# A hand-written opening order with x in half PSUM tiles, and two later due times around the first mixer

## The chip, the cores and the metric

The kernel runs on one core of a Trainium2 chip. The metric is the device time of one execution in microseconds (us). Before the change three runs took 948.01, 948.50 and 948.53 us, median 948.50. The core's engines are TensorE (PE; its weight loads are listed apart as PEld), VectorE (DVE), ScalarE (ACT), GpSimd (POOL) and SyncE (SP), which issues most DMA transfers. Each engine takes its own instructions strictly in the order in which the program lists them; a semaphore makes an instruction, and all that stand behind it on its engine, wait for a result of another engine or for a DMA.

## The reference, cut to what matters

Two layers over x (256 tokens x 1024), each a half-step feed-forward network, a mixer, and a second half-step feed-forward network:

```python
for i in range(2):
    h = rmsnorm(x, ffn1_norm[i])
    x = x + 0.5 * (silu(h @ w_gate) * (h @ w_up)) @ w_down          # D_FF = 2816
    h = rmsnorm(x, mix_norm[i])
    q_s, k_s, v_s, q_m = split(h @ w_in[i])                         # 12 + 12 + 12 + 4 heads of 64
    k_m, v_m = split(rmsnorm(mem, mem_norm[i]) @ w_mem_kv[i])       # memory keys and values
    q, k = rmsnorm(q_s, ...), rmsnorm(k_s, ...)                     # per head; the same for q_m, k_m
    o_s = chunked attention with bias (i = 0) or differential attention with rotary (i = 1)
    o_m = softmax(q_m k_m^T / 8) v_m
    x = x + concat(o_s, o_m) @ w_out[i]
    x = x + 0.5 * swiglu(rmsnorm(x, ffn2_norm[i]), ...)             # as the first
```

All of it is float32, to float32 accuracy.

## The kernel before, in words

**Arithmetic.** Each float32 operand is split in two: `hi`, its rounding to the type fp32r (a copy on ACT), and `lo`, the rest (a subtraction on DVE). A float32 product is three matmuls: hi·xh (line 542), lo·xh (545) and hi·xl (548), in `dense`. The left operand is x transposed, 128 features by 128 tokens (`xh`, `xl`), the right one a weight block of 128 x 512.

**Weights.** `loader` brings them from DRAM in chunks of 128 x 2048 (four k-tiles of 128 x 512), each into one of three `raw` buffers, by DMAs on SP's queue (line 321). `split_hi` (line 367) and `split_lo` (line 385) make `hi` and `lo` from them, into four pairs of buffers. The chunks are called W0, W1, W2, ... here, in order of use. W0 comes in eight pieces, W1 in four, each later gate/up chunk in two of 512 KB. The items of W0 and W1 are split k-tile by k-tile, later gate/up items two k-tiles at a time (`w` in `Item`). W0, W1 and W2 hold 24 matmuls each: four k-tiles, two blocks of 128 tokens, three matmuls. W36 to W39 are the weights of the memory keys and values, W40 and W41 those of the first query/key block of `w_in` in layer 0, W42 and W43 its value block, W44 and W45 its second query/key block.

**Order of the work.** A planner in the kernel's Python (`Flow`) sets it at build time: it keeps an expected time of PE (`flow.now`) and of ACT, DVE and POOL, and runs generators that issue an instruction when its inputs are expected to be there. `yield flow.now + 5.0` means: expect this in 5 us. The result is a fixed list for each engine; the expected times exist only while it is built. A step expected too early stands too early in the list, and its engine then waits at it.

**The opening** (lines 1751 to 1787). x is 2 blocks of tokens (`tb`) by 2 halves of 512 features (`hf`). `start(tb, hf, t)` puts `prep_half` into the plan: four transposes by PE into one PSUM tile (line 578), a scaling by the norm's gain on DVE over 128 x 512 (line 612), the rounding on ACT (line 650: `xh`), the rest on DVE (line 654: `xl`). `start_gain` transposes the gain row (line 1762; tile `gps`, copied to `gcol` at line 1764). `warm(n)` puts matmuls without use on PE (line 1778), of the 128 x 128 identity, which POOL makes first. `square` and `prep_rstd` compute the norm's factor for each token, needed first at the evacuation of the first gate/up block (line 728).

**The first mixer.** `memory_kv` projects the memory keys, normalises them (`kmn`), turns them with a DVE transpose and a round trip through DRAM (`kb` to `kd`, back as `kr`, SP lines 1064 and 1069) and splits them into `km`: two ACT instructions (line 1192) and four DVE ones (line 1195) for each layer. `proj(0)` makes the first query/key block in PSUM tiles `pj`. `head_norm` squares it on ACT (line 1040), sums on DVE (`hss`), takes a power on POOL (`hf`, line 585) and scales on DVE (`qkn`, line 1049). `qk_evac` then turns `qkn` on PE into the tile `qktp` (line 578). Scores are the tile `S` (line 1487), softmax is `pe`, its transposes `ptp`, the product with the values `AV`, and the output projection `acc`. POOL meanwhile works through some ninety small operations for the rotary tables of layer 1 (`ropew`), which end in two sines on ACT (lines 1281 and 1282) and an exponential (line 1321); DVE's `ropeC`, `ropeS` and `nlam` need those.

Of the kernel before, what the change touches and what calls it, by code (L numbers as in the profile page):

```python
# [12 lines left out]
F32 = mybir.dt.float32  # L13
# [28 lines left out]
T_TR = 0.107  # L42
SLACK = 0.4
AHEAD = 0


class Flow:
# [10 lines left out]
        (self.idle if idle else self.threads).append([self.now, gen])  # L58

    def pe(self, dur):  # L60
        self.now += dur
        return self.now + HOP

    def eng(self, e, dur):
# [103 lines left out]
def kernel(  # L168
# [10 lines left out]
    nc = tc.nc  # L179
# [23 lines left out]
    def bank(name, shape=(P, 4, P)):  # L203
        return banks.take(list(shape), F32, name)
# [67 lines left out]
    class Item:  # L272
# [3 lines left out]
        def __init__(self, raws, uses=8, w=1):  # L276
            self.raws, self.uses = raws, uses
            self.hi = self.lo = None
            self.hit, self.lot, self.st = [None] * 7, [None] * 7, [None] * 4
            self.n, self.frees, self.takes, self.gives, self.guest = 1, 1, 0, 0, False  # L280
            self.sums, self.t = [], []
            self.index = len(items)
            w = 1 if len(items) < 2 else w
            self.units = [(self.own(q, w), q, w, None) for q in range(0, 4, w)]
            items.append(self)

# [25 lines left out]
    def loader():  # L312
        for i, c in enumerate(chunks):
            yield lambda: raw_left[0] > 0
            raw_left[0] -= 1
            c.raw = wraw.tile([P, 2048], F32, tag="raw", name=f"raw{i}")
            dma_free[0] = max(dma_free[0], flow.now)
            n = len(c.parts)
            lat = LAT + slow[0] if i > 1 else 0.6
            for j, (dst, src) in enumerate(c.parts):  # L320
                (nc.scalar if i == 0 and j == 1 else nc.sync).dma_start(out=dst(c.raw), in_=src)
                dma_free[0] += 3.0 / n
                if i < 2 and j % 2:
                    for q in range((j - 1) * 4 // n, (j + 1) * 4 // n):
                        c.block[q] = dma_free[0] + lat
# [4 lines left out]
            c.arrive = dma_free[0] + lat  # L330
# [17 lines left out]
    def split_hi():  # L348
        for i, it in enumerate(items):
            yield lambda: (hl_left[0] >= it.n and all(r.raw is not None for r in it.raws)  # L350
                           and (xt_room[0] or not it.guest))
            hl_left[0] -= it.n
            if it.guest:
                xt_room[0] = False
            yield max(r.block[0] for r in it.raws)
            it.hi, it.lo = ([whl.tile([P, 2048], F32R, tag=x, name=f"{x}{i}_{j}") for j in range(it.n)]
                            for x in ("hi", "lo"))
            if it.guest:
                for x, ts in (("xh", it.hi), ("xl", it.lo)):
                    ts += [xtp.tile([P, KT, P], F32R, tag=f"{x}{j}", name=f"g{x}{j}") for j in range(2)]  # L360
            for src, q, w, dep in it.units:
                yield max(r.arrive if dep is not None else r.block[q + w - 1] for r in it.raws)
                if dep is not None:
                    yield lambda: it.st[dep] is not None
                    yield it.st[dep]
                yield calm_a(i)
                nc.scalar.copy(out=it.part(0, q, w), in_=src())  # L367
                t = flow.act(512 * w)
                it.hit[q:q + w] = [t] * w

    def split_lo():
        for i, it in enumerate(items):
            if it.sums:
                yield lambda: all(r.raw is not None for r in it.raws) and g2.left >= it.takes + 2
                yield max(r.arrive for r in it.raws)
                it.t += [g2.take([P, 512], F32, "wsum") for _ in range(it.takes)]
                for j, (x, y) in enumerate(it.sums):
                    yield calm_v(i)
                    nc.vector.tensor_sub(it.t[j], x(), y())  # L379
                    it.st[j] = flow.dve(512)  # L380
            for src, q, w, dep in it.units:
                yield lambda: it.hit[q] is not None
                yield it.hit[q]
                yield calm_v(i)
                nc.vector.tensor_sub(it.part(1, q, w), src(), it.part(0, q, w).bitcast(F32))  # L385
# [84 lines left out]

    def plan_ffn(l, nm, wg, wu, wd):
        def parts(g, c):
            pieces = (4, 2)[len(chunks)] if len(chunks) < 2 else 1
            a = cols4(wg[l], c, g * 256, 256, 0, pieces)
            b = cols4(wu[l], c, g * 256, 256, 256, pieces)
            return [q for ab in zip(a, b) for q in ab]
# [680 lines left out]
    def memory_kv(l):  # L1157
# [7 lines left out]
        def evac(ps, tb, t):  # L1165
            yield t
            nat = yield from head_norm(ps[:, 0:256], 4, mrs[tb], "kmn")
            nc.scalar.activation(vm[:, tb, :], ps[:, 256:512], AF.Copy, scale=mrs[tb])
            kvt[1][tb] = flow.act(256)
            banks.give()  # L1170
            if tb == 0:
                yield g2.has()
                kb.append(g2.take([P, 4, 2, 2, 32], F32, "kb"))
            else:
                yield lambda: len(kb) > 0
            t = turn_blocks(kb[0][:, :, tb], nat)
            g2.give()
            yield t
            done.append(tb)
            if len(done) < 2:  # L1180
                return
            d = through_dram(kb[0], "kd", 2)
            yield flow.now + 4.0
            g2.give()
            yield g2.has()
            r = from_dram(d, "kr")
            yield flow.now + 5.0
            for pr in range(2):
# [3 lines left out]
                nc.scalar.activation(hi, src, AF.Copy, scale=g)  # L1192
                yield flow.act(256)
                for j in range(2):
                    nc.vector.scalar_tensor_tensor(out=lo[:, j], in0=src[:, j], scalar=g, in1=hi.bitcast(F32)[:, j],
                                                   op0=ALU.mult, op1=ALU.subtract)
                    t = flow.dve(128, 0.06)
            g2.give()
            kvt[0][0] = kvt[0][1] = t
# [128 lines left out]
    def mixer(l, xt, gc_next):  # L1328
# [40 lines left out]
        def qk_evac(c):  # L1369
            def run(ps, tb, t):  # L1370
# [5 lines left out]
                if not typ_a:  # L1376
# [379 lines left out]
    flow.step()  # L1756
    xt = Xt(PAIR[0, 1] is not None)

    def start_gain():
        yield 3.9  # L1760
        tp = bank("gps0")
        nc.tensor.transpose(out=tp[:, 0, :16], in_=g1row, identity=ident[:16, :16])
        yield flow.pe(T_TR)
        nc.vector.tensor_copy(gcol[:, 0:16], tp[:, 0, :16])
        banks.give()
        flow.dve(16)
        first_gain.append(True)
        warm(2)
        yield 5.6
        warm(1)  # L1770

    def start(tb, hf, t):
        yield t
        yield from prep_half(xt, tb, hf, GC_FFN1, 3.0)

    def warm(n):
        for _ in range(n):
            nc.tensor.matmul(out=wb[:, 0, :], lhsT=ident, rhs=ident, start=True, stop=True)

    wb = bank("warm")  # L1780
# [69 lines left out]
```

## Time and profile before

| what | value |
|---|---|
| median of three runs | 948.50 us |
| the profiled execution, its own time | 948.83 us |
| its span, first to last instruction | 947.0 us |
| PE, DVE, ACT, POOL busy | 940.3, 829.7, 590.8, 108.6 us |
| DVE subtractions of weights, line 385, from raw | 466 in 392.2 us |
| DMA read from HBM, mean rate | 190.04 MB, 217 GB/s |

The profiled execution took 1.8 us more than its span; what is said of a place in the span carries over to the time one for one. In the rows of the timeline the columns are the start and the length in us, the engine, the line, the operation, out<-in, shapes and count, and in brackets the idle time before it and what ended it. Matmuls overlap: a row's length holds the way through the array, so the pace is read from start to start.

### The profile page before, as it was taken

What the parts mean: (1) busy time and instruction counts of PE and PEld (TensorE: products, weight loads), DVE (VectorE), ACT (ScalarE), POOL (GpSimd) and SP (SyncE); (2) the same over time, 40 slices, a digit from 0 to 9 for tenths busy, and PEclk for the clock granted to TensorE, in tenths of its full rate; (3) what the DMA queues carried; (4) which work ended last, traced back from release to release, by engine and by line L of the source; (5) the groups of instructions that cost most, each with busy time, mean ns of one, the idle gap of its engine ahead of it and who ended that gap; (6) DMA issues with size and microseconds to landing.
All of it is one profiled execution on the core that took longest, in us unless ns stands there. A gap on an engine that the chain in (4) does not pass through costs nothing. (4 is left out here: it accounts for less than half of the span.)

```text
span 947.0 us, 13323 instructions
## 1 busy us (share of the span) xinstructions
PE 940.3 (99%) x4456; PEld 773.2 (82%) x4456; DVE 829.7 (88%) x1501; ACT 590.8 (62%) x1126; POOL 108.6 (11%) x160
## 2 busy tenths in 40 slices
PE   9999999999999999999999999999999999999998
PEld 7888888887878888888888888888887788888887
DVE  6989988888777889989889899796999899998995
ACT  6656666677786746647546656563777765655671
POOL 0000038731210000000000000000334100000000
PEclk9999999999999999999999999999999999999999
DMA  9968799688525486896847679775632367589561
GB/s 296 284 212 250 228 325 329 231 268 254 178 90 164 121 258 210 266 291 225 259 143 217 214 233 290 236 252 173 203 130 76 131 219 225 188 260 329 183 217 47
DMA packets 172574, 206.13 MB, mean 218 GB/s; under 512 B 10265, under 2 KB 147290, under 8 KB 172506
## 3 DMA queue, kind: packets, MB, share of 16 engines
q1 hardware_dynamic: 169498, 202.92, 67.0%
q10 hardware_dynamic: 3008, 2.37, 0.8%
q8 instruction: 35, 0.57, 0.2%
q14 instruction: 33, 0.27, 0.1%
HBM read 190.04 MB, written 15.20 MB: 217 GB/s over the span
## 5 line engine op out<-in xcount | busy, mean ns | idle before, releaser
L367 ACT CAST hi<-raw 128x512 fp32r<-128x512 f32 (+1 forms) x466 | 334.8, 770 | 152.4 <-DMA raw<-in_ffn_w_up_dram 45.7
L385 DVE TENSOR_TENSOR lo<-raw,hi 128x512 fp32r<-128x512 f32 (+1 forms) x466 | 392.2, 877 | 23.1 <-ACT hi L367 22.5
L548 PE MATMUL gu<-hi,xl 128*128 128x512 f32 x528 | 206.0, 390 | 0.0
L542 PE MATMUL gu<-hi,xh 128*128 128x512 f32 x528 | 206.0, 390 | 0.0
L545 PE MATMUL gu<-lo,xh 128*128 128x512 f32 x528 | 205.8, 390 | 0.0
L545 PEld LDWEIGHTS gu<-lo,xh 128*128 128x128 f32 x528 | 99.2, 188 | 21.0 <-DVE lo L385 0.4
L548 PEld LDWEIGHTS gu<-hi,xl 128*128 128x128 f32 x528 | 99.3, 188 | 21.0 <-DVE xl L654 0.4
L542 PEld LDWEIGHTS gu<-hi,xh 128*128 128x128 f32 x528 | 99.4, 188 | 20.4
L548 PE MATMUL acc<-hi,ht 128*128 128x512 f32 x270 | 105.6, 391 | 0.0
L542 PE MATMUL acc<-hi,ht 128*128 128x512 f32 x270 | 105.1, 389 | 0.0
L545 PE MATMUL acc<-lo,ht 128*128 128x512 f32 x270 | 105.1, 389 | 0.0
L367 ACT CAST hi<-wsum 128x512 fp32r<-128x512 f32 x83 | 49.0, 620 | 40.0 <-DVE wsum L379 37.0
L548 PE MATMUL pj<-hi,xl 128*128 128x512 f32 x160 | 63.9, 400 | 0.0
L545 PE MATMUL pj<-lo,xh 128*128 128x512 f32 x160 | 63.6, 397 | 0.0
L542 PE MATMUL pj<-hi,xh 128*128 128x512 f32 x160 | 63.5, 397 | 0.0
L545 PEld LDWEIGHTS acc<-lo,ht 128*128 128x128 f32 x270 | 50.7, 188 | 10.6
L542 PEld LDWEIGHTS acc<-hi,ht 128*128 128x128 f32 x270 | 50.7, 188 | 10.4
L548 PEld LDWEIGHTS acc<-hi,ht 128*128 128x128 f32 x270 | 50.7, 188 | 10.4
L585 POOL TENSOR_TENSOR xr<-v,nhalf 128x1 f32<-128x1 f32 x12 | 8.6, 719 | 429.6 <-DVE v L583 429.6
L385 DVE TENSOR_TENSOR lo<-wsum,hi 128x512 fp32r<-128x512 f32 x83 | 53.7, 676 | 0.0
L728 ACT ACTIVATE sil<-gu,xr 128x256 f32<-128x256 f32 x72 | 33.8, 469 | 24.7 <-PE gu L548 23.1
L585 POOL TENSOR_TENSOR hf<-v,nhalf 128x8 f32<-128x8 f32 (+1 forms) x20 | 32.1, 1607 | 83.2 <-DVE v L583 74.1
(244 smaller groups left out, 1531.5 us busy)
## 6 DMA issues: line engine op xcount, KB each, us to landing
raw<-in_ffn_w_down_dram SPq DMA_DIRECT2D x176, 256.0 KB, 4.4
raw<-in_ffn_w_gate_dram SPq DMA_DIRECT2D x82, 512.0 KB, 4.6
raw<-in_ffn_w_up_dram SPq DMA_DIRECT2D x82, 512.0 KB, 5.2
raw<-in_w_in_dram SPq DMA_DIRECT2D x32, 512.0 KB, 5.1
hd<-hb SPq DMA_DIRECT2D x44, 256.0 KB, 4.9
hr<-hd SPq DMA_DIRECT2D x44, 256.0 KB, 5.1
raw<-in_w_out_dram SPq DMA_DIRECT2D x8, 1024.0 KB, 4.9
raw<-in_w_mem_kv_dram SPq DMA_DIRECT2D x4, 1024.0 KB, 9.0
```

The costliest lines, as they stand in the source:

```text
L367: nc.scalar.copy(out=it.part(0, q, w), in_=src())
L385: nc.vector.tensor_sub(it.part(1, q, w), src(), it.part(0, q, w).bitcast(F32))
L542: nc.tensor.matmul(out=ps, lhsT=xh, rhs=wh, start=start, stop=False)
L545: nc.tensor.matmul(out=ps, lhsT=xh, rhs=wl, start=False, stop=False)
L548: nc.tensor.matmul(out=ps, lhsT=xl, rhs=wh, start=False, stop=stop)
L585: nc.gpsimd.tensor_tensor(out=dst, in0=v[:, :n], in1=nhalf[:, :n], op=ALU.pow)
L728: nc.scalar.activation(sil, ps[tb][:, 0:256], AF.Silu, scale=xt.r[tb])
```

## The change

Four things. (1) The opening's instructions are written out in order by hand: the warm matmuls use a zeroed tile of 128 x 128 bf16 that DVE clears, 23 of them ahead of the gain's transpose; the first half of x's first block is turned into two PSUM tiles of two k-tiles each (A and B), and scaled, rounded and subtracted in these halves; the second block's first half (C) stays whole. The planner gets a table of arrival times (`FIRST`) for the first three chunks, doubles PE's cost up to 7.5 us, and leaves the three `hi` and two `lo` that are now written by hand. The squares for the norm start in the plan at 18 us or later. (2) W2 comes in four pieces and is split k-tile by k-tile. (3) The memory keys are expected back 9 us after their load instead of 5. (4) In layer 0 each transpose of q and k is due 2 us later.

```diff
     def pe(self, dur):
-        self.now += dur
+        self.now += dur * (2 if self.now < COLD else 1)
         return self.now + HOP
...
-            w = 1 if len(items) < 2 else w
+            w = 1 if len(items) < 3 else w
...
+    FIRST = ((4.7, 6.1, 6.9, 8.6), (10.2, 10.2, 12.1, 12.1), (15.1, 15.1, 16.6, 16.6))
...
             for src, q, w, dep in it.units:
+                if i == 0 and q < 3:
+                    continue
...
             for src, q, w, dep in it.units:
+                if i == 0 and q < 2:
+                    continue
...
-            pieces = (4, 2)[len(chunks)] if len(chunks) < 2 else 1
+            pieces = (4, 2, 2)[len(chunks)] if len(chunks) < 3 else 1
...
             r = from_dram(d, "kr")
-            yield flow.now + 5.0
+            yield flow.now + 9.0
...
                     yield flow.dve(512)
+                if typ_a and True:
+                    yield flow.now + 2.0
                 yield banks.has()
                 tp = bank("qktp")
...
-    warm(5)
-    flow.now = 2.7
-    flow.spawn(start_gain())
+    wz = junk[:, 0:P]
+    nc.vector.memset(wz, 0.0)
...
+    warm(23)
+    tp = bank("gps0")
+    nc.tensor.transpose(out=tp[:, 0, :16], in_=g1row, identity=ident[:16, :16])
+    nc.vector.tensor_copy(gcol[:, 0:16], tp[:, 0, :16])
+    warm(2)
     for tb in range(2):
-        for hf in range(2):
-            flow.spawn(start(tb, hf, (3.4, 12.6, 5.8, 13.4)[2 * tb + hf]))
+        xt.y[tb, 0] = g2.take([P, 4, P], F32, "y")
+        flow.spawn(square(xt, tb, 0, 18.0))
+    A, B, C = (0, 1), (2, 3), range(4)
+    flow.now = 4.0
+    tpa, tpb = turned(0, A), turned(0, B)
+    first_hi(0)
+    scaled(0, tpa, A)
+    high(0, A)
+    scaled(0, tpb, B)
+    first_lo(0)
+    high(0, B)
+    low(0, A)
+    warm(4)
+    flow.now = 5.35
+    tpc = turned(1, C)
+    first_hi(1)
+    scaled(1, tpc, C)
+    low(0, B)
+    first_hi(2)
+    high(1, C)
+    first_lo(1)
+    low(1, C)
+    for tb, t in ((0, 13.2), (1, 14.0)):
+        flow.spawn(start(tb, t))
```

Here `turned` issues transposes, `scaled` the gain on DVE, `high` the rounding on ACT, `low` the subtraction on DVE, `first_hi(q)` and `first_lo(q)` the split of W0's k-tile q; `start` now prepares only the second half of features.

What the lists become, at the places of which the prediction speaks. The lists of all engines differ up to the end of the first mixer (PE's up to row 1420 of some 4300, counted one instruction a row) and are the same from there on.

VectorE's first instructions, before (`raw_110`, `hi_0_164` and `lo_0_165` are W0; `xl_133` and `xl_134` are the two blocks of tokens):

```order
L1764 COPY gcol<-gps_157 128x16
L612 TENSOR_TENSOR y<-xtp,gcol 128x512
L385 TENSOR_TENSOR lo_0_165<-raw_110,hi_0_164 128x512
L654 TENSOR_TENSOR xl_133<-y,xh_131 128x512
L612 TENSOR_TENSOR y<-xtp,gcol 128x512
L385 TENSOR_TENSOR lo_0_165<-raw_110,hi_0_164 128x512 x2
L654 TENSOR_TENSOR xl_134<-y,xh_132 128x512
```

VectorE's first instructions, now (W0 is `raw_110`, `hi_0_121`, `lo_0_122`; `xl_137` and `xl_138` are the blocks; lines are those of the changed file):

```order
L1769 MEMSET junk 128x64
L1816 COPY gcol<-gps_168 128x16
L1786 TENSOR_TENSOR y<-xtp,gcol 128x256 x2
L1806 TENSOR_TENSOR lo_0_122<-raw_110,hi_0_121 128x512
L1798 TENSOR_TENSOR xl_137<-y,xh_135 128x256
L1786 TENSOR_TENSOR y<-xtp,gcol 128x512
L1798 TENSOR_TENSOR xl_137<-y,xh_135 128x256
L1806 TENSOR_TENSOR lo_0_122<-raw_110,hi_0_121 128x512
L1798 TENSOR_TENSOR xl_138<-y,xh_136 128x512
```

Three subtractions of W0 stood ahead of the second block's `xl`, now two; the first block's scaling and `xl` are in halves, of which the first needs two transposes only.

VectorE ahead of the first `qkn`, before (`lo43` and `lo44` are W43 and W44, `km0` the memory keys of layer 0):

```order
L1043 TENSOR_REDUCE hss_2302<-sq_2292 128x8
L583 TENSOR_SCALAR v_2305<-hss_2302 128x8
L1195 SCALAR_TENSOR_TENSOR km0_1979<-kr_2252,gcol_103,km0_1979 128x128 x4
L385 TENSOR_TENSOR lo43_0_2258<-raw40_2209,hi43_0_2257 128x512 x2
L385 TENSOR_TENSOR lo44_0_2317<-raw41_2243,hi44_0_2316 128x512
L1049 SCALAR_TENSOR_TENSOR qkn_2343<-pj0_2229,xr_1816,hf_2304 128x512
```

And now:

```order
L1050 TENSOR_REDUCE hss_2333<-sq_2324 128x8
L590 TENSOR_SCALAR v_2336<-hss_2333 128x8
L392 TENSOR_TENSOR lo43_0_2290<-raw40_2240,hi43_0_2289 128x512 x2
L392 TENSOR_TENSOR lo44_0_2346<-raw41_2277,hi44_0_2345 128x512 x2
L1298 SCALAR_TENSOR_TENSOR ropeC_107<-gqk_208,ropew_1438 128x32
L1300 SCALAR_TENSOR_TENSOR ropeS_108<-gqk_208,ropew_1438 128x32
L1056 SCALAR_TENSOR_TENSOR qkn_2373<-pj0_2261,xr_1836,hf_2335 128x512
L1202 SCALAR_TENSOR_TENSOR km0_1999<-kr_2266,gcol_103,km0_1999 128x128 x4
```

The four `km` have moved from ahead of `qkn` to behind it; one more subtraction of W44 and two short `rope` steps stand ahead of it.

TensorE around the first `qktp`, before (`pj1` with hi41 is the end of the first query/key block, `pj0` with hi42 the first half of the value block):

```order
L548 MATMUL pj1_2230<-hi41_0_2143,xl1_1813 128x512
L542 MATMUL pj0_2350<-hi42_0_2202,xh0_1810 128x512
L545 MATMUL pj0_2350<-lo42_0_2203,xh0_1810 128x512
L548 MATMUL pj0_2350<-hi42_0_2202,xl0_1812 128x512
...
L578 MATMUL qktp_2364<-flip_98,qkn_2343 128x128 x2
L578 MATMUL qktp_2364<-ident_88,qkn_2343 128x128 x2
```

And now (hi43 is the second half of the value block):

```order
L555 MATMUL pj0_2380<-hi42_0_2234,xl0_1832 128x512
L549 MATMUL pj0_2380<-hi43_0_2289,xh0_1830 128x512
L552 MATMUL pj0_2380<-lo43_0_2290,xh0_1830 128x512
L555 MATMUL pj0_2380<-hi43_0_2289,xl0_1832 128x512
L549 MATMUL pj0_2380<-hi43_0_2289,xh0_1830 128x512
L585 MATMUL qktp_2420<-flip_98,qkn_2373 128x128 x2
L585 MATMUL qktp_2420<-ident_88,qkn_2373 128x128 x2
```

Before, 54 `pj` matmuls (48 of the query/key block and 6 of the value block) stand ahead of the first `qktp`; now 64 (48 and 16). Later in the mixer the first scores `S` come behind 110 `pj` instead of 95, and between them and the first `ptp` stand 18 instead of 24.

More of the change, by code (lines that the diff above doesn't have):

```diff
@@ L44 @@
 AHEAD = 0
+COLD = 7.5
 class Flow:
@@ L322, in loader @@
                 dma_free[0] += 3.0 / n
-                if i < 2 and j % 2:
+                if i < 3 and j % 2:
                     for q in range((j - 1) * 4 // n, (j + 1) * 4 // n):
-                        c.block[q] = dma_free[0] + lat
+                        c.block[q] = FIRST[i][q]
                 if i == 0 and j == 1:
@@ L329, in loader @@
                     dma_free[0] += 0.75
-            c.arrive = dma_free[0] + lat
+            c.arrive = dma_free[0] + lat if i > 2 else FIRST[i][3]
             c.block = [t or c.arrive for t in c.block]
@@ L354, in split_hi @@
                 xt_room[0] = False
-            yield max(r.block[0] for r in it.raws)
+            if i:
+                yield max(r.block[0] for r in it.raws)
             it.hi, it.lo = ([whl.tile([P, 2048], F32R, tag=x, name=f"{x}{i}_{j}") for j in range(it.n)]
@@ L1757 @@
     xt = Xt(PAIR[0, 1] is not None)
[L1759 to L1774, printed above, removed]
+    wz = junk[:, 0:P]
@@ L1776, in warm, with turned, scaled @@
+    nc.vector.memset(wz, 0.0)
+    wb = bank("warm")
+    banks.give()
     def warm(n):
         for _ in range(n):
-            nc.tensor.matmul(out=wb[:, 0, :], lhsT=ident, rhs=ident, start=True, stop=True)
-    wb = bank("warm")
+            nc.tensor.matmul(out=wb[:, 0, :], lhsT=wz, rhs=wz, start=True, stop=True)
+    def turned(tb, ks):
+        tp = bank("xtp")
+        for k in ks:
+            turn(tp[:, k - ks[0], :], xs[tb][:, k * P:(k + 1) * P])
+        return tp
+    def scaled(tb, tp, ks):
+        n = len(ks)
+        g = gcol[:, GC_FFN1 + ks[0]:GC_FFN1 + ks[0] + n]
+        nc.vector.tensor_tensor(out=xt.y[tb, 0][:, ks[0]:ks[0] + n], in0=tp[:, 0:n],
+                                in1=g.unsqueeze(2).broadcast_to([P, n, P]), op=ALU.mult)
+        banks.give()
+        flow.dve(n * P)
@@ new lines, in high, with low, first_hi @@
+    def high(tb, ks):
+        sl = slice(ks[0], ks[0] + len(ks))
+        nc.scalar.copy(out=xt.h[tb][:, sl, :], in_=xt.y[tb, 0][:, sl])
+        xt.th[tb][sl] = [flow.act(P * len(ks))] * len(ks)
+    def low(tb, ks):
+        sl = slice(ks[0], ks[0] + len(ks))
+        nc.vector.tensor_sub(xt.l[tb][:, sl, :], xt.y[tb, 0][:, sl], xt.h[tb].bitcast(F32)[:, sl, :])
+        xt.t[tb][sl] = [flow.dve(P * len(ks))] * len(ks)
+    def first_hi(q):
+        nc.scalar.copy(out=items[0].part(0, q), in_=items[0].own(q)())
+        items[0].hit[q] = flow.act(512)
@@ L1781, with first_lo, start @@
+    def first_lo(q):
+        nc.vector.tensor_sub(items[0].part(1, q), items[0].own(q)(), items[0].part(0, q).bitcast(F32))
+        items[0].lot[q] = flow.dve(512)
+    def start(tb, t):
+        yield t
+        yield from prep_half(xt, tb, 1, GC_FFN1, 3.0)
+    warm(23)
+    tp = bank("gps0")
+    nc.tensor.transpose(out=tp[:, 0, :16], in_=g1row, identity=ident[:16, :16])
+    nc.vector.tensor_copy(gcol[:, 0:16], tp[:, 0, :16])
     banks.give()
-    warm(5)
-    flow.now = 2.7
-    flow.spawn(start_gain())
+    warm(2)
@@ L1785 @@
+    first_gain.append(True)
     for tb in range(2):
-        for hf in range(2):
-            flow.spawn(start(tb, hf, (3.4, 12.6, 5.8, 13.4)[2 * tb + hf]))
+        xt.y[tb, 0] = g2.take([P, 4, P], F32, "y")
[3 more added lines that the diff above has]
+    tpa, tpb = turned(0, A), turned(0, B)
+    flow.free.update(A=4.75, V=4.75)
+    first_hi(0)
[4 more added lines that the diff above has]
+    high(0, B)
@@ L1788 @@
+    low(0, A)
+    warm(4)
+    flow.now = 5.35
+    tpc = turned(1, C)
+    flow.free["A"] = 6.1
+    first_hi(1)
+    scaled(1, tpc, C)
+    low(0, B)
+    flow.free["A"] = 6.85
+    first_hi(2)
[4 more added lines that the diff above has]
+        flow.spawn(start(tb, t))
     flow.spawn(gain_columns())
```

## The prediction

> **What bounds the kernel now.** I read the page's part 1 first, then the busy time in stretches of 100 us, then TensorE's own waits, then the timeline at the places those name.
>
> ```profile
> PE 940.3 (99%) x4456; PEld 773.2 (82%) x4456; DVE 829.7 (88%) x1501; ACT 590.8 (62%) x1126; POOL 108.6 (11%) x160
> ```
> ```profile
> 100.00:200.00 100.00, 100.00 (x442) 82.78 (x442) 88.06 (x168) 68.31 (x139) 51.94 (x102) 1.00 0.89 292
> 200.00:300.00 100.00, 98.89 (x583) 79.81 (x582) 82.84 (x230) 73.56 (x183) 17.67 (x12) 1.00 0.55 176
> ```
> ```profile
> PE qktp L578 <- DVE qkn L1049: 1.1, 1, 1.1
> ```
>
> PE is busy for 99% of the span, at the full granted clock. The first stretch is pure matmul: 442 in 100 us, 0.226 us from start to start. That pace is my unit. In the second stretch 1.11 us are missing, and the waits name the owner: the first transpose of q and k, `qktp`, waits 1.1 us for VectorE's `qkn`. So nothing is to be had in the middle of the kernel; there is only the opening and this one wait. The opening:
>
> ```profile
> 4.01 1.11 PE L578 MATMUL xtp<-ident,x 128*128 128x128 f32 x4 [0.15 <-DMA x<-in_x_dram]
> 4.72 0.62 ACT L367 CAST hi<-raw 128x512 fp32r<-128x512 f32 x1 [1.57 <-DMA raw<-in_ffn_w_up_dram]
> 5.27 1.65 PE L1778 MATMUL warm<-ident 128*128 128x128 f32 x6
> 5.38 0.17 DVE L1764 COPY gcol<-gps 128x16 f32<-128x16 f32 x1 [5.38 <-PE gps L1762]
> 5.58 0.69 DVE L612 TENSOR_TENSOR y<-xtp,gcol 128x512 f32<-128x512 f32 x1
> 6.19 0.68 DVE L385 TENSOR_TENSOR lo<-raw,hi 128x512 fp32r<-128x512 f32 x1
> 6.31 0.62 ACT L650 CAST xh<-y 128x512 fp32r<-128x512 f32 x1 [0.97 <-DVE y L612]
> 6.50 0.87 PEld L578 LDWEIGHTS xtp<-ident,x 128*128 128x128 f32 x4
> 7.42 0.78 PE L542 MATMUL gu<-hi,xh 128*128 128x512 f32 x1
> 8.42 0.63 PE L548 MATMUL gu<-hi,xl 128*128 128x512 f32 x1
> 8.85 0.45 PE L542 MATMUL gu<-hi,xh 128*128 128x512 f32 x1
> 9.62 0.69 DVE L654 TENSOR_TENSOR xl<-y,xh 128x512 fp32r<-128x512 f32 x1
> 10.36 0.50 PE L548 MATMUL gu<-hi,xl 128*128 128x512 f32 x1
> 10.70 0.40 PE L542 MATMUL gu<-hi,xh 128*128 128x512 f32 x1
> ```
>
> x is there at 4.01, but the first useful matmul starts at 7.42. The scaling `y` had to wait for the gain column (5.38), which PE had transposed only after x. The second block's `xl` (9.62, ended 10.31) stood behind three subtractions of W0, and the ninth matmul (10.36) waited for it. After the tenth, at 10.70, PE goes on at its pace. So the start of the tenth is the mark: whatever makes it earlier is gained once and kept, if nothing behind it is late.
>
> **The change, the opening.** The gain is now transposed ahead of x, so `y` needs only two transposes, half of 1.11 us: 4.01 + 0.55 and a hand-over of 0.1 gives 4.67. A half tile costs VectorE and ScalarE about
>
> ```profile
> L1579 DVE TENSOR_TENSOR oT<-AV,oT 128x256 fp32r<-128x256 f32 x10 | 4.2, 418 | 2.8 <-ACT oT L1577 2.8
> L785 ACT CAST h<-hr 128x256 fp32r<-128x256 f32 x10 | 4.0, 401 | 1.5 <-DMA hr<-hd 1.5
> ```
>
> 0.42 and 0.40 us, so the two halves cost VectorE 0.84 where a whole took 0.69: 0.15 more for each of the two steps cut, on the engine that sets this stretch. VectorE's list, each from its predecessor's end: `y` A and B to 5.51, `lo` of k-tile 0 to 6.19, `xl` A to about 6.6, `y` C to 7.3, `xl` B to 7.6, `lo` of k-tile 1 to 8.29, `xl` C to about 8.9. ScalarE ends what these need in time: `hi` at 5.34, `xh` A at 5.74 and B at 6.14, two more `hi` to 7.5, `xh` C at 8.1. On PE the first matmul starts behind C's transposes, near 6.6; the fifth needs `lo` of k-tile 1, 8.29; the ninth needs `xl` C, 8.9.
>
> The pace there is a matter of the clock. The rows 8.42 and 8.85 are 0.43 apart, 10.36 and 10.70 only 0.34 with a wait's end in it, so near 8.9 the pace goes from 0.43 to 0.23, though the granted clock's column says 1.00 throughout. If it changes at the same time again, the fifth starts at 8.29, the seventh near 9.1 and the tenth at 9.74: 0.96 earlier than 10.70. If it has changed before 8.3, the tenth starts at 8.29 + 5 x 0.23 = 9.44: 1.26 earlier. I take 1.1, between them, since the warm matmuls start earlier and are more.
>
> In the trace the clock came 3.6 us after the second warm stretch began (5.27 to 8.9), with transposes in between. The Trainium skill, "TensorE: Matmul & The Clock Gate", section "What's actually happening", says that the clock is full after one busy window of about 3.4 us, and that the windows run freely; its section "Part 4: PE-mode transpose" says that transposes do not count as busy in the same way. By the first rule alone the sum would use 1.26; by both, strictly, a window without transposes could not end before about 10, and the sum would use 0.26. The row lies with the first: the dense stretch alone was 1.5 us old at 8.9.
>
> One arrival is not shown: x's first half of block 1, which C needs.
>
> ```profile
> x<-in_x_dram SPq DMA_DIRECT2D x1, 256.0 KB, 3.2
> x<-in_x_dram SPq DMA_DIRECT2D x4, 256.0 KB, 4.4
> ```
>
> The first load of x took 3.2 us, the median of the four 4.4. The second was issued at 1.65, so it lands at 4.9 or 6.05; the PEld row at 6.50, PE's own list position, is the latest. At 4.9 the sum stands as above. At 6.05 C ends some 0.4 later, and 0.55 is left of the gain; at 6.50, 0.1. I take 4.9, since the row for the load next to it in the queue is the 3.2.
>
> Behind the tenth matmul nothing should be late:
>
> ```profile
> 10.76 0.63 ACT L667 ACTIVATE junk<-x 128x512 bf16<-128x512 f32 x1
> 16.47 2.00 ACT L367 CAST hi<-raw 128x1024 fp32r<-128x1024 f32 x2
> 20.57 1.23 DVE L385 TENSOR_TENSOR lo<-raw,hi 128x1024 fp32r<-128x1024 f32 x1 [0.39 <-ACT hi L367]
> ```
>
> W2 in k-tiles costs ScalarE 4 x 0.62 for 2.00, 0.5 more, and VectorE 4 x 0.69 for 2 x 1.23, 0.3 more. The four squares, 0.63 each, now stand together ahead of W3's first `hi`. ScalarE: W2 done at about 18.9, squares to 21.4, W3's `hi` 1.05 more, VectorE's `lo` 1.23 more: 23.7. PE comes to W3 with its 73rd matmul; 63 paces of 0.228 and two breaks of transposes (0.9) behind the tenth is 25.9 before and 24.8 now. Cost nothing, with 1.1 us in hand; each microsecond beyond that would cost one.
>
> **Memory keys and margin.** The first mixer:
>
> ```profile
> 217.33 0.17 DVE L583 TENSOR_SCALAR v<-hss 128x8 f32<-128x8 f32 x1
> 217.58 1.64 POOL L585 TENSOR_TENSOR hf<-v,nhalf 128x8 f32<-128x8 f32 x1 [4.03 <-DVE v L583]
> 218.47 1.14 DVE L1195 SCALAR_TENSOR_TENSOR km<-kr,gcol,km 128x128 fp32r<-128x128 f32 x4 [0.97 <-ACT km L1192]
> 219.53 1.89 DVE L385 TENSOR_TENSOR lo<-raw,hi 128x512 fp32r<-128x512 f32 x3
> 220.63 0.39 PE L548 MATMUL pj<-hi,xl 128*128 128x512 f32 x1
> 221.34 0.74 DVE L1049 SCALAR_TENSOR_TENSOR qkn<-pj,xr,hf 128x512 f32<-128x512 f32 x1
> 222.13 0.44 PE L578 MATMUL qktp<-flip,qkn 128*128 128x128 f32 x2 [1.11 <-DVE qkn L1049]
> ```
>
> VectorE waits 0.97 us for ScalarE's half of `km`; then come four `km`, three `lo`, and only then `qkn`, which ends 22.08 past 200. PE ended its last `pj` pace at 220.86 and started `qktp` at 222.13: 1.27 us lost.
>
> Now VectorE has at this place, from `v`'s end at 217.5: four `lo` of 1.89/3 = 0.63, which overlap a little (219.9) and two rope steps of about 0.1 (220.1); POOL's `hf` ends at 219.22. So `qkn` runs to 220.85. PE has 64 `pj` ahead of `qktp` instead of 54, 10 x 0.226 = 2.3 us more useful work, and comes at 220.86 + 2.26 = 223.1. That is 2.2 us of slack, and the 1.27 goes away wholly. Either edit alone would do: without `km`'s detour `qkn` ends in time, and with the ten matmuls PE comes 1.0 behind the end of the old `qkn`. Behind `qktp` on PE stand the further `pj` and `S`; the `pj` are only exchanged in order. What becomes late next is `S`, below. Nobody on PE needs `km` until the scores of the memory heads, far behind.
>
> The profiled execution took 948.83: 948.83 - 1.1 - 1.27 = 946.46. It stood 0.33 above the median of 948.50, so 946.1 on the scale of the medians.
>
> **The rivals.** *The opening gives little.* x lands at 6.05 or later, or the clock comes later because transposes do not count: the gain is 0.1 to 0.55. At 0.3 the time is 948.5 - 0.3 - 1.27 = 946.9. For it: the median row of x. Against: the 3.2 row.
>
> *A wait moves into attention.* The delay also moves the scores.
>
> ```profile
> 232.52 0.72 PE L1487 MATMUL S<-qk 64*128 64x128 f32 x8
> 237.93 0.88 DVE L1552 TENSOR_SCALAR pe<-pe,rs 128x128 f32<-128x128 f32 x4
> 239.46 0.38 PE L578 MATMUL ptp<-flip,pe 128*128 128x128 f32 x2
> ```
>
> Softmax took 238.81 - 232.52 = 6.29 us from `S` to the end of `pe`, and `ptp` came 0.65 after that. `S` stands behind 15 more `pj` (3.4 us, less the lost 1.27: 2.1 later), with 18 instead of 24 `pj` between it and `ptp`; six fewer is 1.36 us, so the distance of 6.94 becomes 5.58, 0.7 short of the 6.29. If the chain is no quicker, PE waits 0.7 here and in one more group, 1.0 to 1.4 for both: 947.1 at 1.0. Against it: part of the 6.29 was ScalarE serving `hi` in between, and it has more time now.
>
> *POOL is late* (the slower side). The rope steps on POOL wait in one list with the powers that memory keys need.
>
> ```profile
> 191.79 0.95 POOL L585 TENSOR_TENSOR xr<-v,nhalf 128x1 f32<-128x1 f32 x1 [1.36 <-DVE v L583]
> 195.89 0.26 ACT L1281 ACTIVATE ropew<-ropew 128x64 f32<-128x64 f32 x1
> 198.12 0.20 ACT L1321 ACTIVATE le<-le 128x2 f32<-128x2 f32 x1
> 200.53 1.32 POOL L585 TENSOR_TENSOR hf<-v,nhalf 128x4 f32<-128x4 f32 x1 [1.58 <-DVE v L583]
> 208.62 0.39 PE L542 MATMUL pj<-hi,xh 128*128 128x512 f32 x1
> ```
>
> Before, two `ropew` steps stood behind the second `xr`, now fourteen, four of them behind the second `hf`. A step takes 51.94/102 = 0.51 and some 0.08 to the next: the last ends at 201.85 + 4 x 0.59 = 204.2 instead of before 195.9. The sine, then the exponential 2.2 later, stand on ScalarE ahead of W42; VectorE's `nlam` waits for the exponential ahead of `lo` of W41, which PE needs at 208.62 + 12 x 0.226 = 211.3. The exponential ends at about 206.5 and two `lo` follow by 208.1: hidden, with some 3 us in hand. If the steps took 1.15 us each instead of 0.59, 8 us later in all, PE would stand 5 us, and the time would be 946.1 + 5 = 951.1. The point where it decides is 3 us late; the point where it makes the kernel slower by more than 1.9 us, about 7.5 late.
>
> **How the numbers follow.** The chances: forecast 0.55, little from the opening 0.20, wait in attention 0.17, POOL 0.08. The predicted time is the forecast's, 946.1, whose own range is 945.7 to 946.8 (gain of 0.4 to 1.5 us in the opening: at the upper end a clock that is full early and a VectorE 0.2 quicker). The two middle cases end at 946.9 and 947.1, both together at 947.9. The range of 945.3 to 948.1 adds to these the scatter of the runs of before, some 0.4 below and 0.2 above, and leaves out the POOL case. About 0.2% (1.9 us) is what a measurement can tell from no change: faster means under 946.6, which takes most of the forecast (0.47 of 0.55) and a fifth of the middle cases (0.07); slower means over 950.4, three quarters of the POOL case: 0.54, 0.40 and 0.06.
>
> **What would show it.** In the profile after: the tenth dense matmul at 9.4 to 9.8; the wait of `qktp` for `qkn` gone from PE's waits, `qkn` ended 2 us before `qktp`; 200 to 300 us of PE full but for 0.1; no new PE wait on `ptp` for `pe` (attention), on W41's `lo` (POOL) or on W3's `lo` (squares). A tenth at 10.1 or later says that x or the clock came late; a PE wait on `ptp` of 0.5 or more that the margin cost what it gave. A time above 948.1 would mean that a mechanism was missed.

## The result: 4.2 us slower, and the profile after

| | median of 5 runs | profiled execution | its span |
|---|---|---|---|
| before | 948.53 us (948.01 to 949.37) | 948.83 us | 947.0 us |
| after | 952.73 us (952.48 to 954.22) | 952.73 us | 950.9 us |

The ratio is 1.0042, with a 95% interval of 1.0030 to 1.0053. Forecast were 946.1 us and a range of 945.3 to 948.1.

The busy times of two stretches after (columns: the stretch and its length, busy time and number of instructions of PE, PEld, DVE, ACT and POOL, granted clock, DMA share, GB/s), and TensorE's waits:

```profile
100.00:200.00 100.00, 98.87 (x429) 79.55 (x428) 88.46 (x164) 64.84 (x134) 45.51 (x91) 1.00 0.85 283
200.00:300.00 100.00, 98.94 (x572) 79.49 (x571) 84.47 (x237) 76.03 (x189) 23.56 (x24) 1.00 0.56 179
```
```profile
PE gu L552 <- DVE lo L392: 1.2, 3, 0.9
PE qktp L585 <- DVE qkn L1056: 1.0, 1, 1.0
...
PE pair_m L552 <- DVE lo L392: 0.6, 1, 0.6
```

The stretch from 100 to 200 us was full before; now it lacks 1.1 us, and two waits stand in the list that before did not have: `gu` and `pair_m` (matmuls of the first feed-forward network) wait for the subtraction `lo` of their weights. The wait of `qktp` is still there, 1.0 instead of 1.1. The list counts only time in which TensorE shows nothing at all, and a row's length holds the way through the array; read from start to start, what exceeds the pace between 79 and 127 us adds up to 4.5 us, all but 0.3 of it at nine matmuls that take a `lo` of line 392 and at the one right behind each.

To see where each microsecond goes I number the 128 x 512 matmuls in TensorE's order and compare the start of the k-th in two profiles (each trace has 3852 of them; inside the mixer their order differs, past it they can be compared again). Behind the change at k = 10 the kernel is 1.1 us ahead, and still at k = 250 (66 us of before). At k = 500 (123 us) it is 3.3 us behind, at k = 881 (210 us) 3.5, past the mixer (k = 1300) 3.8, and so to the end. So the opening gave 1.1; then 4.4 to 4.6 us were lost between 79 and 127 us of the span, in a network whose code was not touched; the mixer gave nothing and lost another 0.3.

**The opening**, timeline of after:

```profile
7.15 0.44 PE L555 MATMUL gu<-hi,xl 128*128 128x512 f32 x1
7.43 0.47 PE L549 MATMUL gu<-hi,xh 128*128 128x512 f32 x1
8.21 0.50 PE L552 MATMUL gu<-lo,xh 128*128 128x512 f32 x1 [0.32 <-DVE lo L1806]
...
9.29 0.49 PE L555 MATMUL gu<-hi,xl 128*128 128x512 f32 x1
...
9.63 0.39 PE L549 MATMUL gu<-hi,xh 128*128 128x512 f32 x1
```
```profile
8.55 0.69 DVE L1798 TENSOR_TENSOR xl<-y,xh 128x512 fp32r<-128x512 f32 x1 [0.39 <-ACT xh L1793]
```

The fifth matmul starts at 8.21 behind `lo` of k-tile 1 (forecast 8.29), the tenth at 9.63 (9.4 to 9.8; 10.70 before). The pace is fast from about 7.2 on, 1.7 us earlier than before. The ninth (9.29) stands behind `xl` C, which ended at 9.24 because ScalarE's `xh` C was 0.4 us later than forecast.

**The loss.** W12, W14, W15, W16 and W17 are chunks of the first network. There are three raw buffers; W17 goes into the one that holds W12, whose last reader is the second half of a `lo`. First before, by queue and engine (SP rows are load issues; W16's is the first, W17's the second, the first of its eight: W8, W10, W12 and W17 come in eight pieces of 128 KB, as W0 does):

```profile
78.44 0.37 SPq L321 DMA_DIRECT2D raw<-in_ffn_w_gate_dram  x1
...
80.70 0.35 SPq L321 DMA_DIRECT2D raw<-in_ffn_w_gate_dram  x1
```
```profile
76.06 4.62 DVE L385 TENSOR_TENSOR lo<-raw,hi 128x1024 fp32r<-128x1024 f32 x4
...
83.47 0.68 DVE L894 TENSOR_TENSOR gu_v<-gu_u,pair_m 128x512 f32<-128x512 f32 x1
```

Four `lo` in a row end at 80.68, the fourth frees W12's buffer, W17 is issued at 80.70, and only then come the four `gu_v`. After:

```profile
80.66 0.37 SPq L323 DMA_DIRECT2D raw<-in_ffn_w_gate_dram  x1
...
86.00 0.35 SPq L323 DMA_DIRECT2D raw<-in_ffn_w_gate_dram  x1
```
```profile
78.28 3.49 DVE L392 TENSOR_TENSOR lo<-raw,hi 128x1024 fp32r<-128x1024 f32 x3
...
82.40 2.01 DVE L901 TENSOR_TENSOR gu_v<-gu_v,pair_m 128x512 f32<-128x512 f32 x3
84.33 0.48 DVE L738 SCALAR_TENSOR_TENSOR h<-gu,xr,sil 128x256 f32<-128x256 f32 x1
84.72 1.22 DVE L392 TENSOR_TENSOR lo<-raw,hi 128x1024 fp32r<-128x1024 f32 x1
...
88.56 0.48 DVE L738 SCALAR_TENSOR_TENSOR h<-gu,xr,sil 128x256 f32<-128x256 f32 x1 [1.16 <-ACT sil L735]
88.96 1.22 DVE L392 TENSOR_TENSOR lo<-raw,hi 128x1024 fp32r<-128x1024 f32 x1
```
```profile
86.16 2.00 ACT L372 CAST hi<-raw 128x1024 fp32r<-128x1024 f32 x2 [3.29 <-DMA raw<-in_ffn_w_up_dram]
88.06 0.47 ACT L735 ACTIVATE sil<-gu,xr 128x256 f32<-128x256 f32 x1
```
```profile
90.23 0.50 PE L552 MATMUL gu<-lo,xh 128*128 128x512 f32 x1 [0.86 <-DVE lo L392]
```

The fourth `lo` now stands behind the four `gu_v` and an `h`; it starts at 84.72 and W17 is issued at 86.00, 5.3 us later than before although TensorE is 1.1 us earlier. W16 is 2.2 us later as well (80.66). ScalarE waits for it in both kernels, but here until 86.16 and before until 84.09; `sil` stands behind that wait, `h` behind `sil`, the next `lo` behind `h`, and TensorE gets it 0.86 us late. It goes on so to 127 us, shortly ahead of the network's down projection (130.5). The lag is older than this place: W12's own load was issued at 56.39, for 50.29 before.

**The mixer**, timeline of after:

```profile
225.77 0.74 DVE L1056 SCALAR_TENSOR_TENSOR qkn<-pj,xr,hf 128x512 f32<-128x512 f32 x1
...
230.60 3.10 DVE L392 TENSOR_TENSOR lo<-raw,hi 128x512 fp32r<-128x512 f32 x5
233.62 0.74 DVE L1056 SCALAR_TENSOR_TENSOR qkn<-pj,xr,hf 128x512 f32<-128x512 f32 x1
```
```profile
226.93 0.38 PE L585 MATMUL qktp<-flip,qkn 128*128 128x128 f32 x2
...
234.51 0.41 PE L585 MATMUL qktp<-flip,qkn 128*128 128x128 f32 x2 [1.03 <-DVE qkn L1056]
```

The first `qkn` ends at 226.51, 0.4 us ahead of its `qktp`: that wait is gone. The second one waits 1.03 us. Five subtractions stand ahead of the second `qkn`, but they alone don't make it late: in e9 below, with the same lists and loads that come in time, it ends at 226.57 and its `qktp` comes at 229.51 without a wait. VectorE came late to this place. A smaller loss stands ahead of it:

```profile
213.15 0.16 DVE L1330 SCALAR_TENSOR_TENSOR nlam<-le 128x1 f32<-128x1 f32 x1 [1.21 <-ACT le L1328]
```
```profile
217.28 0.50 PE L552 MATMUL pj<-lo,xh 128*128 128x512 f32 x1
```

VectorE waits 1.21 us for the exponential `le`; the subtractions behind it come later, and the 23rd `pj`, which needs the last `lo` of W41, starts 0.18 us late and the one behind it 0.11.

### The profile page after: what moved, and what is told of

Read it like the earlier page. It is cut to its first block, busy times and chain, and to the rows that moved or that the text cites. A ratio compares the mean times of both kernels' runs of the same rounds, so it can differ in the third digit from the quotient of the medians.

```text
span 950.9 us, 13354 instructions
## 1 busy us (share of the span) xinstructions
PE 942.3 (99%) x4469; PEld 771.6 (81%) x4469; DVE 828.2 (87%) x1506; ACT 591.2 (62%) x1129; POOL 108.5 (11%) x160
## 5 line engine op out<-in xcount | busy, mean ns | idle before, releaser
L738 DVE SCALAR_TENSOR_TENSOR h<-gu,xr,sil 128x256 f32<-128x256 f32 x72 | 34.4, 478 | 12.5 <-ACT sil L735 12.5
```

The lines of the kernel that those rows point to most:

```text
L738: nc.vector.scalar_tensor_tensor(out=h, in0=ps[tb][:, 256:512], scalar=xt.r[tb], in1=sil, op0=ALU.mult, op1=ALU.mult)
```

## The experiments

Theory S: the four squares of the norm, which now stand together ahead of W3's split, set the splits back, and with three raw buffers the lag lives on in late loads. Theory W: W2 in four pieces does it. Theory M: the two edits of the mixer do.

The times are medians; each run was compared with runs of the kernel before on the same chip (948.97, 948.77 and 948.71 us in the three groups). The columns on the right are TensorE's place against the profile of before, in us, minus being ahead.

| kernel | time | k = 10 | 250 | 500 | 881 | 1300 |
|---|---|---|---|---|---|---|
| after | 952.73 | -1.1 | -1.1 | 3.3 | 3.5 | 3.8 |
| e1 squares early | 947.25 | -1.4 | -1.5 | -1.4 | -1.4 | -1.3 |
| e2 W2 in two | 953.66 | -1.4 | -1.5 | 3.5 | 3.5 | 4.7 |
| e3 opening alone | 955.99 | -1.2 | -1.2 | 5.3 | 5.4 | 8.0 |
| e4 mixer alone | 947.28 | -0.1 | -0.2 | -0.2 | -0.2 | -1.4 |
| e5 before, squares late | 951.40 | -0.3 | -0.3 | -0.3 | -0.3 | 1.8 |
| e6 e1 and e2 | 946.25 | -1.2 | -1.3 | -1.3 | -1.3 | -2.5 |
| e7 short squares | 953.80 | -1.5 | -1.5 | 5.0 | 5.2 | 5.2 |
| e8 e1 without mixer edits | 950.32 | -1.5 | -1.4 | -1.4 | -1.4 | 1.4 |
| e9 after, four raw buffers | 946.70 | 0.1 | 0.0 | 0.0 | 0.0 | -1.2 |
| e10 e6, four raw buffers | 946.36 | -1.3 | -1.4 | -1.4 | -1.4 | -2.6 |
| e11 memory keys alone | 947.19 | -0.3 | -0.4 | -0.4 | -0.4 | -1.3 |
| e12 margin alone | 948.63 | -0.2 | 0.0 | 0.0 | 0.0 | -0.5 |

**e1, the squares early.** In the changed kernel:

```diff
-        flow.spawn(square(xt, tb, 0, 18.0))
+        flow.spawn(square(xt, tb, 0, 10.0 + 2.5 * tb))
```

> The changed kernel, with the squares of x's first halves planned at 10.0 and 12.5 us as the kernel before has them, instead of 18. Theory S (the four squares stand together on ScalarE ahead of W3's split, the splitting of the weights falls some 2 us behind, raw buffers come free later, loads start later, and TensorE meets the lag at 88 to 127 us, 4.6 us in all): most of the 4.6 goes, about 948.3 us, no wait of gu or pair_m for lo between 85 and 130 us. Theory W (W2 in four pieces is what lags) and theory M (the two edits of the mixer cost it): 952 or more, waits as in the changed kernel.

947.25 us (ratio to before 0.9984, 0.9973 to 0.9995): 5.5 us less than after from one line (eleven of its twelve runs took 946.29 to 948.24, one 952.83; why that one did is not known). The place of W17's load again, in SP's queue and on VectorE:

```profile
82.10 0.35 SPq L323 DMA_DIRECT2D raw<-in_ffn_w_gate_dram  x1
```
```profile
79.71 2.36 DVE L392 TENSOR_TENSOR lo<-raw,hi 128x1024 fp32r<-128x1024 f32 x2
81.98 0.68 DVE L901 TENSOR_TENSOR gu_v<-gu_u,pair_m 128x512 f32<-128x512 f32 x1
```
```profile
PE qktp L585 <- DVE qkn L1056: 0.8, 1, 0.8
```

Both halves of the `lo` stand ahead of `gu_v` again, the load is issued 3.9 us earlier, W12's is issued at 53.72 (56.39 in after), and of the waits for `lo` of later weights none is left. The one for `qkn` is.

**e2, W2 in two pieces.** In the changed kernel:

```diff
-            w = 1 if len(items) < 3 else w
+            w = 1 if len(items) < 2 else w
-            pieces = (4, 2, 2)[len(chunks)] if len(chunks) < 3 else 1
+            pieces = (4, 2)[len(chunks)] if len(chunks) < 2 else 1
-    FIRST = (..., (15.1, 15.1, 16.6, 16.6))
+    FIRST = (..., (16.6, 16.6, 16.6, 16.6))
```

> The changed kernel, with W2 loaded in two pieces and split two k-tiles at a time as before. Theory W: the lag of the splits goes, about 948.3 us. Theory S: the squares still stand together ahead of W3, 952 to 953 us with waits of gu and pair_m for lo between 85 and 130 us.

953.66 us (1.0053, 1.0042 to 1.0065), 5.0 us lost between k = 250 and 500. Theory W falls.

**e3, the opening alone.** The changed kernel without `+ 2.0` and with `+ 5.0` for the memory keys.

> The changed kernel without its two edits to the mixer (memory keys back after 5 us, no margin): the opening alone. Theory M: 949 or less. Theory S: the lag up to 127 us is there unchanged, +3.5 us at that point, and the old wait of 1.3 us at the first q and k transpose is back or moved: 952 to 953 us.

955.99 us (1.0066, 1.0051 to 1.0081), slower than expected. The lists up to the mixer are those of after, yet 6.5 us are lost there instead of 4.4 to 4.6: the size of this loss is not fixed by the lists. In the mixer another 2.5 are lost, with two waits of `qktp`:

```profile
PE qktp L585 <- DVE qkn L1056: 2.9, 2, 2.0
```

So theory M falls too: in this company the mixer's edits save 2.2 us (2.5 lost there against 0.3 in after).

**e4, the mixer's edits alone**, in the kernel before:

```diff
-            yield flow.now + 5.0
+            yield flow.now + 9.0
...
+                if typ_a and True:
+                    yield flow.now + 2.0
                 yield banks.has()
                 tp = bank("qktp")
```

> The kernel before with the two edits to the mixer alone (memory keys expected after 9 us, 2 us more ahead of the q and k transposes of layer 0). If the prediction's term was right, 1.27 us less, 947.2 us, with no wait of qktp. If VectorE's queue of weight subtractions makes the next transpose late instead, as the changed kernel shows (1.0 us at the second qktp), 948.0 to 948.8 us with a wait of about 1 us at a later qktp. Theory M (these edits are what costs): 952.

947.28 us (0.9982, 0.9973 to 0.9990), 1.2 us gained at the place.

```profile
219.76 0.73 DVE L1049 SCALAR_TENSOR_TENSOR qkn<-pj,xr,hf 128x512 f32<-128x512 f32 x1
```
```profile
222.98 0.39 PE L578 MATMUL qktp<-flip,qkn 128*128 128x128 f32 x2
```

`qkn` ends at 220.49 and TensorE comes 2.5 us later. Here nothing waits at the second transposes either.

**e5, the squares late in the kernel before:**

```diff
-            flow.spawn(square(xt, tb, hf, flow.now + wait))
+            flow.spawn(square(xt, tb, hf, max(18.0, flow.now + wait)))
```

> The kernel before with one line changed: the squares of the first network stand at 18 us or later, so that all four come together ahead of W3's split, as in the changed kernel; opening and mixer as before. Theory S: the lag comes without the opening, waits of gu or pair_m for lo between 75 and 130 us, 951 to 953.5 us. Rival (the lag needs the new opening, W2 in four or an earlier TensorE): 948.5 to 949.5, no such waits.

951.40 us (1.0028, 1.0017 to 1.0039): the time that theory S gave, and not its place. Nothing is lost up to k = 881; in its profile (950.65 us) 2.2 us go in the mixer, where both `qktp` now wait:

```profile
PE qktp L578 <- DVE qkn L1049: 3.7, 2, 2.5
```

So late squares alone don't make the lag. It needs the new opening as well, and in the form "squares set back the splits" theory S falls. What both kernels share is that four small steps put elsewhere reorder lists hundreds of instructions later.

**e6, e1 and e2 together.**

> The changed kernel with the squares at 10.0 and 12.5 us and W2 in two pieces; its instruction lists in the mixer are then those of the kernel with the mixer's edits alone. If the opening (1.1 to 1.5 us) and the mixer (1.25 us) add up when the lists agree: 946.0 to 946.6 us, no wait of qktp. If the mixer's gain is lost whenever the opening is early: 947.2.

946.25 us (0.9971, 0.9961 to 0.9982), the fastest here: 1.3 from the opening and 1.2 from the mixer in its profile, no wait of `qktp`. With the mixer's lists of e4 the gains add up. Against e1 the second `qktp` no longer waits.

**e7, short squares**, in the changed kernel, for the first network:

```diff
+        n = 512 if len(short) > 3 else 16
+        short.append(1)
-        nc.scalar.activation(junk, xs[tb][:, hf * 512:(hf + 1) * 512], AF.Square,
+        nc.scalar.activation(junk[:, 0:n], xs[tb][:, hf * 512:hf * 512 + n], AF.Square,
```

> The changed kernel with its instruction lists unchanged, but the four squares of the first network sum 16 columns instead of 512 each (so the norm's factor leaves out most of x). Told apart: whether the lag is the 2.5 us that the squares really hold ScalarE, or the places that the planner gave the later steps because it reckoned with them. If the time on ScalarE is it (duration): about 948 us, no waits of gu and pair_m for lo between 85 and 130 us. If the fixed order is it: 951.5 to 953, the waits remain.

953.80 us (1.0050, 1.0037 to 1.0063). A square takes 0.21 us instead of 0.63, ScalarE's timeline:

```profile
18.07 0.21 ACT L678 ACTIVATE junk<-x 128x16 bf16<-128x16 f32 x1
...
20.70 2.00 ACT L372 CAST hi<-raw 128x1024 fp32r<-128x1024 f32 x2 [1.30 <-DMA raw<-in_ffn_w_up_dram]
```
```profile
PE gu L552 <- DVE lo L392: 1.9, 5, 0.8
```

ScalarE now is free 1.3 us before W3 arrives, and the loss is as large as ever (6.5 us). The time that the squares take is not the cause. The order is, which the planner made because it reckoned with them.

**e8, e1 without the mixer's edits.**

> The changed kernel with the squares at 10.0 and 12.5 us and without the two edits to the mixer. With them it took 947.25. If the mixer's edits gain what the trace of before shows at the first q and k transpose: 948.5. If they gain what they gained between the opening alone and the changed kernel (some 3 us, waits at two transposes): 949.5 to 950.5. If they gain nothing here: 947.3.

950.32 us (1.0016, 1.0007 to 1.0024). Opening and network are as in e1; the mixer loses 2.8 us where e1 loses nothing, with one wait of `qktp` of 2.9 us. The new opening alone turns the first mixer's wait from 1.1 into 2.9 us. The wait is not the whole of it in this profile, since TensorE is slow behind it:

```profile
222.53 0.44 PE L585 MATMUL qktp<-flip,qkn 128*128 128x128 f32 x2 [2.93 <-DVE qkn L1056]
...
223.41 0.63 PE L552 MATMUL pj<-lo,xh 128*128 128x512 f32 x1
223.84 0.63 PE L555 MATMUL pj<-hi,xl 128*128 128x512 f32 x1
...
226.67 0.39 PE L549 MATMUL pj<-hi,xh 128*128 128x512 f32 x1
```
```profile
222.00:227.00 5.00, 4.47 (x15) 3.61 (x16) 4.97 (x10) 3.81 (x8) 1.84 (x1) 0.66 0.96 300
```

Eight matmuls stand 0.43 us apart instead of 0.23, and the column of the granted clock shows 0.66 for the stretch: some 1.6 us. So the 2.8 us of this profile, which took 950.54, are the wait and a slow clock together, and the agreement with the expectation is in part chance.

**e9, a fourth raw buffer**, in the changed kernel. The planner still reckons with three, so every list is the same:

```diff
-    wraw = ctx.enter_context(tc.tile_pool(name="wraw", bufs=NRAW))
+    wraw = ctx.enter_context(tc.tile_pool(name="wraw", bufs=4))
-    t2 = ctx.enter_context(tc.tile_pool(name="t2", bufs=NT2))
+    t2 = ctx.enter_context(tc.tile_pool(name="t2", bufs=15))
```

> The changed kernel, instruction lists of all engines unchanged, but with four raw buffers for the weights instead of three (four of the nineteen half-size scratch tiles, which are never all in use, make room), so that a load no longer waits for the last subtraction of the chunk three before it. Theory B (in the changed order that subtraction stands late on VectorE, behind four gu_v, so the load starts late and TensorE meets it at 88 to 127 us): the waits for lo there go, about 948.3 us. Rival (the lag is made by the order on ScalarE and VectorE itself, whatever the loads do): 951.5 to 953.

946.70 us (0.9981, 0.9972 to 0.9990), 6.0 us less than after. SP's queue and VectorE:

```profile
80.35 0.35 SPq L323 DMA_DIRECT2D raw<-in_ffn_w_gate_dram  x1
```
```profile
84.41 1.21 DVE L392 TENSOR_TENSOR lo<-raw,hi 128x1024 fp32r<-128x1024 f32 x1
```

The `lo` stands as late as in after (84.41), but W17 is issued at 80.35 without it. No wait for a `lo` is left anywhere, and none of `qktp` either. Theory B stands: the loss is loads that wait for a buffer whose last reader was put late. It took 1.6 us less than theory B gave, since the mixer gains 1.2 us here as well, with the lists of after. Its profile is one with a late opening (below), which leaves the loads more time; but its eleven runs took 946.25 to 947.90, so none of them has the loss.

**e10, e6 with a fourth raw buffer.**

> The fastest version so far (squares early, W2 in two pieces, 946.25 us) with four raw buffers, lists unchanged. No wait of TensorE for weights is left in it, so both theories expect no change, 945.9 to 946.5 us; more would mean that late loads cost TensorE where the waits do not show them.

946.36 us (0.9976, 0.9967 to 0.9985): no change, as expected. Here, where the order frees the buffers in time, a fourth is worth nothing.

**e11 and e12, each edit of the mixer alone**, in the kernel before (the first and the second part of e4's diff).

> The kernel before with the memory keys expected after 9 us and nothing else. The prediction said that either edit alone would do: VectorE reaches the first qkn about 1.2 us sooner, ended near 220.85, just as TensorE comes (220.86): 947.4 to 947.8 us, a wait of qktp of 0.3 us or less. If the wait only moves to the second transpose: 948.3 to 948.8.

> The kernel before with the 2 us margin alone. By the prediction TensorE comes 2.3 us later, 1.0 behind the end of the old qkn: the first wait goes, 947.4 to 947.6 us. If the memory keys, which then still stand ahead, make the second qkn late: 948.3 to 949 with a wait at the second qktp.

The memory keys alone: 947.19 us (0.9983, 0.9975 to 0.9992), as much as both edits. At the place its profile gains 0.9: the first wait is gone, and half of it comes back at the second transposes:

```profile
227.58 0.41 PE L578 MATMUL qktp<-flip,qkn 128*128 128x128 f32 x2 [0.63 <-DVE qkn L1049]
```

The margin alone: 948.63 us (0.9995, 0.9987 to 1.0004), no difference. `qkn` stays where it was, and TensorE comes after it:

```profile
221.32 0.75 DVE L1049 SCALAR_TENSOR_TENSOR qkn<-pj,xr,hf 128x512 f32<-128x512 f32 x1
```
```profile
223.10 0.38 PE L578 MATMUL qktp<-flip,qkn 128*128 128x128 f32 x2
```

Neither `qktp` waits; some 1.0 of the 1.45 us gained there is given back in the rest of the mixer, between 234 and 290 us, in small losses of which only those about the scores `S` show as waits.

## Why the prediction was wrong

**The opening: right in size, in part by luck.** The tenth matmul came 1.07 us earlier, for 1.1, and `lo` of k-tile 1 ended at 8.16 for 8.29. But the pace turned fast near 7.2, which is the case for which the prediction reckoned 9.44 and a gain of 1.26; the tenth came at 9.63 because the ninth was late. "ScalarE ends what these need in time" was wrong by 0.4 us: it waited 0.71 us for W0's load and ended `xh` C at 8.51 for 8.1, so `xl` C ended at 9.24 for 8.9. Before's opening also varies by itself: in e4, e5, e11 and e12, which have its list, the tenth came 0.1 to 0.3 earlier than in before. In the mean of the five profiles with the old list it starts at 10.5 and of the nine with the new one at 9.5.

**"Behind the tenth matmul nothing should be late": the step that failed.** The prediction followed the squares to W3, found 1.1 us in hand there, put the cost at nothing, and stopped. That much was right, since no matmul of W3 waited. But it asked only when W3's data would be ready, not what the changed order does to the buffers that come free. The lists of all engines differ up to the end of the mixer, which the prediction knew and used for the mixer alone (POOL, `qkn`, the scores). It took "nothing is to be had in the middle of the kernel" for "nothing can be lost there". With 4.4 to 4.6 us lost, this is most of the error of 6.3 us between the profiled executions (3.9 slower for 2.4 faster); the rest is the mixer's 1.27, which did not come, and the 0.3 lost there. e1 shows that the squares' due time makes the order, e7 that it is the order and not their time, e9 that the order costs through the late freeing of raw buffers.

**The wait of `qktp`: right in size, wrong in what stands around it.** 1.27 was forecast. In the kernel for which it was worked out the edits give 1.2 (e4). In the changed kernel the new opening had first made the waits there larger, 2.9 us in both e8 and e3; the edits took most of that away, and against before 0.3 is lost, because VectorE, late from the network on, made the second `qkn` late. With loads in time (e9) the same lists gain 1.2 there. So in after this term failed by the same step as the one above. "Either edit alone would do" held for the memory keys (e11) and failed for the margin (e12), where later steps gave the gain back. The prediction asked about the first transposes and the scores, but not about the second transposes.

**The rivals.** None was the main cause. The place that the POOL rival named did cost something, 0.3 us at W41's last `lo`. POOL itself was not late: its last step of the tables ended at 207.95, with TensorE 3.5 us behind before at that point, so at 204.5 for a forecast 204.2. ScalarE was: the exponential ended at 213.11, so at 209.6 for 206.5, and the prediction had put the point where it decides at 3 us. The scores' chain was not late: no `ptp` waits. An opening that gives little did come, in one profile: e9's, whose lists in the opening are those of after.

```profile
5.92 1.11 PE L585 MATMUL xtp<-ident,x 128*128 128x128 f32 x4 [0.48 <-DMA x<-in_x_dram]
...
9.77 0.63 PE L549 MATMUL gu<-hi,xh 128*128 128x512 f32 x1
...
10.75 0.39 PE L549 MATMUL gu<-hi,xh 128*128 128x512 f32 x1
```

There x came at 5.92 instead of 5.38, the slow pace lasted to 10.2, and the tenth started at 10.75: nothing gained. The median of its runs, 946.70, is 1.2 below the time of that profiled execution (947.9), so most of its runs were faster than the one profiled. So after's own lists come to within 0.6 us of the forecast 946.1 once loads don't wait for buffers.

**What stays open.** Which part of the new opening it is that, with late squares, puts the fourth `lo` behind `gu_v`: W2's pieces are ruled out (e2), arrival table, hand order and the times at which the planner takes ScalarE and VectorE to be free (which the change also sets by hand in the opening) were not tried apart. The loss had 4.4 us in after and 6.5 in e3 and e7, whose orders are the same up to the mixer. In e3 the difference can be followed to one load, the second half of W9, issued at 36.79 (36.27 in after); ScalarE gets it 1.8 us later. First after, then e3:

```profile
43.38 1.05 ACT L372 CAST hi<-raw 128x1024 fp32r<-128x1024 f32 x1 [2.56 <-DMA raw<-in_ffn_w_up_dram]
```
```profile
45.18 1.05 ACT L372 CAST hi<-raw 128x1024 fp32r<-128x1024 f32 x1 [4.20 <-DMA raw<-in_ffn_w_up_dram]
```

W12 is then issued at 58.18 for 56.39 and W17 at 89.05 for 86.00. In e7 the same load comes 0.7 late, W12 at 57.06 and W17 at 87.58. Why that load took longer is not shown.

## What to carry to other kernels

Where a program at build time sets the order of all engines, an edit at the start is an edit of everything behind it: compare the lists to where they become equal again, and in each stretch ask not only when data is ready but which instruction is the last reader of each buffer that a load waits for, and whether it has moved. An engine that is busy 99% of the time has nothing to give in the middle, but much to lose. One more buffer, without a change to the order, is a direct test of whether late loads are the cause.

## What the runs showed of the hardware that was not expected

The same list of TensorE in the opening gave a tenth matmul at 9.63 (after) and at 10.75 (e9): the slow pace of 0.43 us ended near 7.2 us in the one and near 10.2 in the other, while the column of the granted clock shows 1.00 throughout in both. The column can't show it, since the trace's records of the granted clock begin only with the change to full, at 7.25 us in after, 10.38 in e9 and 8.96 in before. In the other seven profiles with the new list it stands between 4.33 and 7.22. The Trainium skill, "TensorE: Matmul & The Clock Gate", section "What's actually happening", has the windows run freely, so that the point of change varies from run to run; the traces agree that it varies, but by more than the 0.5 us either way that it names. In e9 x also came 0.54 us later, so for that one profile the two causes are not parted.

A stop in the middle can cost clock as well. In e8 TensorE stood for 2.93 us, and the trace records a granted clock of 0.5 from 223.06 to 226.47, eight matmuls at 0.43 us. In e5 it stood for 2.54 us at the same step, and the matmuls behind it came 0.23 us apart from the second on.
